# A depthwise convolution of eight channel chunks shared out anew: one chunk moves from TensorE to ScalarE and GpSimd

## The chip, the cores and the metric
The kernel runs on one core of one Trainium2 chip. A core has TensorE (PE, matrix products), VectorE (DVE), ScalarE (ACT), GpSimd (POOL) and SyncE (SP, which here only issues DMA transfers). Each engine works through its own list of instructions in order and waits on semaphores for the others. The metric is the device time of one launch in microseconds (us); three runs of the kernel before gave a median of 1120.81 us (1120.72 to 1121.36).

## The reference, cut to what matters
Two layers over x of 512 tokens by 1024 channels, in float32. Layer 0 mixes by a Conformer convolution module, layer 1 by native sparse attention; behind each stands a SwiGLU feed-forward network. What the change touches most is the convolution module:

```python
def conformer_conv_module(h, w_in, b_in, w_dw, b_dw, ln_g, ln_b, w_out):
    a, g = jnp.split(h @ w_in + b_in, 2, axis=-1)
    u = a * jax.nn.sigmoid(g)
    u = lax.conv_general_dilated(
        u, w_dw[:, None, :].astype(u.dtype), window_strides=(1,),
        padding=[(CONV_WIDTH - 1, 0)], dimension_numbers=('NWC', 'WIO', 'NWC'),
        feature_group_count=D_MODEL) + b_dw
    ...
    uf = (uf - mu) * lax.rsqrt(var + LN_EPS) * ln_g.astype(jnp.float32) + ln_b.astype(jnp.float32)
    u = jax.nn.silu(uf).astype(h.dtype)
    return u @ w_out
```

The convolution is depthwise: each of the 1024 channels has 31 taps of its own, output[t] = sum over j of w[j] u[t - 30 + j] plus a bias. Behind it stands a LayerNorm over the channels of each token (mean mu, variance var), then silu and the output product. In attention, the change touches the compressed branch: softmax of the scores against the compressed keys, times a gate, times the compressed values.

## The kernel before, in words
**Products.** A float32 product is done as three TensorE products of split operands: high part by high part, high by low, low by high. A weight tile `wr` comes by DMA from SP's queue (three buffers); ACT copies its rounded high part into `wh`, and DVE subtracts to get the low part `wl` (two buffers each). One tile of the input product is 24 matmuls into a PSUM tile `pp`.

**The convolution stage** (the first 130 us) goes over 8 chunks of 128 channels, laid out as channels by time. The loop over i from 2 to 7 is called "pass i" below. A pass finishes chunk i-1 and computes the input product of chunk i:
- `glu_1(i - 1)`: DVE multiplies the gate half out of PSUM by the RMS factors (`gr`), ACT takes its sigmoid in place, DVE does the same to the other half (`ar`);
- `w_lo(n + 1)`: DVE's `wl` for the second half of this pass; `w_hi` is ACT's `wh`;
- `glu_2(i - 1)`: DVE makes the chunk u = (ar + bias) * gr;
- TensorE multiplies two tiles: `pA` (linear half) and `pG` (gate half) of chunk i.

**The depthwise part has two ways.** Chunks 0 and 1 (`DVE_CONV`) are done by DVE, one instruction per tap, accumulating in a PSUM tile `cv`; the list `TAPS_AT` says how many taps go where in each pass. Chunks 2 to 7 (`PE_CONV`) are done by TensorE: `u` is written to a DRAM buffer `swap` and read back by phase (`uf`, SP's queue), multiplied by banded tap matrices `bd` (80 matmuls a chunk, `cpe`), corrected by `nb` (made on POOL), evicted into `uf` by DVE, squared by ACT and sent back through `swap`. The bands of the first three PE chunks are loaded by POOL's DMA queue at the start (two transfers of 1280 KB each), those of the last three made on POOL by `make_band` (8 instructions of 128x640 each, `bd<-i,wtab`). There are three buffers of bands. In pass 6 TensorE does the bands of chunks 2 and 3, in pass 7 chunk 4, behind the loop chunks 5, 6 and 7.

**LayerNorm sums** run over the channels, so TensorE makes them: `ln_shift` takes the mean of chunk 0 as a shift `s` that all chunks subtract first (`u<-u,s`); `ln_sum` (`lnst`) sums the chunks in time layout and their squares (`lsq`), `ph_sum` and `ph_last` (`lng`) those in phase layout.

**What sets the order.** `pe(...)` fixes an instruction's place in its engine's list, so in this stage each engine works in the order in which the code is written. All of these instructions pass through one helper, so the profile has one line, L153, for nearly everything; they are told apart by their tiles.

**Attention.** `cmp_k` makes the compressed keys and copies four small pieces `kcb` on DVE. `soft_c` finishes the softmax of the first pair of heads: DVE's sum (`cl<-sc`), a reciprocal, the product with the gates (`cl<-cl,gates`) and POOL's scaling (`sc<-sc,cl`). `V_BESIDE` is a table that says which small steps stand beside which block of the value product; `weigh` scales the probabilities `Pm`, mostly on POOL.

Of the kernel before, what the change touches and what calls it, by code (L numbers as in the profile page):

```python
# [19 lines left out]
P = 128  # L20
# [35 lines left out]
PE_CONV = (2, 3, 4, 5, 6, 7)  # L56
LN_ORDER = (0, 1)
BAND_BUFS = 3
LOADED = 3
SPLIT = {7: 2}  # L60
EH = 2
TAPS_AT = {2: (2, 4), 3: (3, 5), 4: (3, 5), 5: (3, 5), 6: (7, 3, 3), 7: (4, 6, 0), 8: (5, 4)}
NLN = len(LN_ORDER)
PH_B = 48
NPH = PH_B + 8 * len(PE_CONV)
# [26 lines left out]
    (("ga", "w", "s0", "s1 b1"), ("", "s2 s3 w", "gb s4 l", "s5 st1"), ("s6 l", "s7 l", "sc", "")))  # L92
# [85 lines left out]
def trunk(ctx: ExitStack, tc: tile.TileContext, A, out):  # L178
# [132 lines left out]
    wtab = cb.tile([P, len(PE_CONV) - LOADED, 320], F32, name="wtab")  # L311
# [158 lines left out]
    def conv_module():  # L470
        acc = new_acc()
        with ExitStack() as cx:
# [112 lines left out]
            def glu_2(i, ar, gr):  # L585
# [6 lines left out]
                if i in PE_CONV[:3]:  # L592
                    ups[i] = conv_pe_load(i)
# [50 lines left out]

            def conv_nb(i):
                j = PE_CONV.index(i)
                nb = cp.tile([P, 8, 64], F32, tag="c", bufs=3, name=f"nb{i}")
                pe(nc.gpsimd.tensor_tensor(
                    nb, ph[:, PH_B + 8 * j:PH_B + 8 * j + 8].unsqueeze(2).to_broadcast([P, 8, 64]),
                    sh["sp"][:, None, :].to_broadcast([P, 8, 64]), ALU.subtract))  # L650
                sh["g", i] = ups[i][:, :, 4:], nb, SPLIT.get(i, 8)
# [13 lines left out]
            def conv_end(i, ps):  # L665
                conv_nb(i)
# [23 lines left out]
            def ln_stat(i):  # L690
                pe(nc.vector.tensor_tensor(vch[i], vt[i], sh["s"], ALU.subtract))
# [20 lines left out]
            def ph_last():  # L712
                ps = sh["G2"] = pm.tile([P, 64], F32, tag="pm", name="lng")
                for g in range(8):
                    for j in (4, 5):
# [8 lines left out]
            def ln_rows():  # L724
                sh["rows"] = ct.tile([P, 8, 64], F32, tag="ptap", name="rows", bufs=3)
# [20 lines left out]
            def ln_end():  # L746

                red = sh["red"]
                pe(nc.vector.tensor_tensor(red, red, sh["G2"], ALU.add))
# [27 lines left out]
            for i in range(2, NK):  # L777
# [4 lines left out]
                glu_2(i - 1, *z)  # L782
                if i == 6:
                    ps = [conv_mm(2, 0, 8)]
                    make_band(3)
                    ps.append(conv_mm(3, 0, 8))
                    taps(c[0])
                    ln_shift(LN_ORDER[0])
                elif i == 7:
                    make_band(4)  # L790
                    for j in range(2):
                        ph_sum(j)
                        ups[5 + j] = conv_pe_load(5 + j)
# [1705 lines left out]
```

## Time and profile before

| | |
|---|---|
| median of three runs | 1120.81 us (1120.72 to 1121.36) |
| the profiled execution | 1120.53 us, its span 1118.8 us, granted TensorE clock 1.00 |
| busy in the span | PE 1111.2 us (99%), DVE 847.1 (76%), ACT 612.8 (55%), POOL 389.9 (35%) |
| convolution stage, chain of waits from 59.93 to 127.66 us | PE pp 47.3%, PE cpe 42.7%, PE lng 4.6%, rest 5.4% |
| POOL in that stage | 24 instructions of `make_band`, 76.1 to 115.8 us; idle from 18 us to 76 us but for its transfers |

A row of the timeline or of the chain reads: start in us, length in us, engine, line, operation, output tile <- input tiles, shape, count, and in brackets the idle time before it with what ended it. A row with x8 is eight instructions in a run. PE records carry modelled ends, so their lengths overlap; the steps between their starts are the pace. In a row of the tiles' view three numbers stand for the shortest, median and longest duration in ns.

### The profile page before, as it was taken

How to read it: one execution, taken by the hardware profiler on the slowest of the kernel's cores; microseconds unless marked ns; L12 is line 12 of the kernel's file. 1: busy time of each engine (PE TensorE's matmuls, PEld its weight loads, DVE VectorE, ACT ScalarE, POOL GpSimd, SP SyncE). 2: the span in 40 equal slices, each digit the busy share in tenths (PEclk: the TensorE clock that was granted, in tenths of full speed). 3: DMA queues.
4: the chain of work that ended last, by engine and by line, in shares of the span. 5: the costliest groups of instructions: out<-in, count | busy, mean ns of one | idle time of the engine just before them, and what ended most of it. 6: DMA issues, size and time to landing. Idle time of an engine off the chain costs nothing.

```text
span 1118.8 us, 21723 instructions
## 1 busy us (share of the span) xinstructions
PE 1111.2 (99%) x8350; PEld 998.1 (89%) x8350; DVE 847.1 (76%) x1569; ACT 612.8 (55%) x1120; POOL 389.9 (35%) x431
## 2 busy tenths in 40 slices
PE   9999999999999999999999999999999999999998
PEld 6888788999999988998789877768889999998898
DVE  7997897998766578875677878764799876657676
ACT  6322475566555465555344688774556655545543
POOL 1029242024444200333243678752302454420041
PEclk9999999999999999999999999999999999999999
DMA  9744428277877532534373132112736787762342
GB/s 361 290 137 126 106 94 226 101 194 210 205 196 199 160 123 95 152 102 116 119 176 116 53 80 54 40 40 94 209 111 177 205 214 197 197 180 96 111 133 76
DMA packets 86551, 164.26 MB, mean 147 GB/s; under 512 B 36656, under 2 KB 37808, under 8 KB 85680
## 3 DMA queue, kind: packets, MB, share of 16 engines
q1 hardware_dynamic: 66800, 108.47, 31.0%
q0 software_dynamic: 19504, 54.37, 20.5%
q8 instruction: 65, 1.06, 0.4%
q14 instruction: 38, 0.31, 0.1%
q10 hardware_dynamic: 144, 0.04, 0.0%
HBM read 147.22 MB, written 5.28 MB: 136 GB/s over the span
## 4 chain that ended last, share of the span: by engine, by line
PE 94%; DVE 3%; ACT 1%; issue 1%; POOL 0%; DMA 0%; SPq 0%; DVEq 0%; POOLq 0%; ACTq 0%
PE st L153 50%; PE pp L153 28%; PE O L153 4%; PE T L153 3%; PE cpe L153 3%; PE S L153 3%; PE pv L153 2%; PE psc L153 1%; DVE Pm L153 1%; ACT hh L153 0%; DMA x<-xT 0%; DVE t L153 0%; PE z L153 0%; DVE wl L153 0%; POOL Pm L153 0%
## 5 line engine op out<-in xcount | busy, mean ns | idle before, releaser
L153 PE MATMUL st<-ball,sh 128*128 128x256 f32 x1760 | 299.7, 275 | 0.0
L153 PEld LDWEIGHTS st<-ball,sh 128*128 128x128 f32 x1760 | 267.5, 192 | 0.3
L153 PE MATMUL st<-ball,sl 128*128 128x256 f32 x880 | 242.3, 275 | 0.0
L153 DVE TENSOR_TENSOR wl<-wr,wh 128x1024 fp32r<-128x1024 f32 (+3 forms) x143 | 178.0, 1245 | 66.3 <-ACT wh L153 66.0
L153 ACT ACTIVATE wh<-wr 128x1024 fp32r<-128x1024 f32 (+4 forms) x144 | 148.6, 1032 | 143.9 <-PE pp L153 57.4
L153 POOL DMA_DIRECT2D S<-fw_x x88 | 78.1, 893 | 279.8 <-DVE sl L153 195.9
L153 PEld LDWEIGHTS st<-ball,sl 128*128 128x128 f32 x880 | 169.2, 192 | 0.0
L153 POOL TENSOR_TENSOR S<-S,wr 128x512 f32<-128x512 f32 x72 | 99.9, 1388 | 142.5 <-DMA wr<-fw_op 115.6
L153 PE MATMUL pp<-hh,wh 128*128 128x512 f32 x384 | 148.8, 388 | 0.1
L153 PE MATMUL pp<-hh,wl 128*128 128x512 f32 x384 | 146.2, 381 | 0.4 <-DVE wl L153 0.3
L153 PE MATMUL pp<-hl,wh 128*128 128x512 f32 x384 | 145.6, 380 | 0.1
L153 ACT ACTIVATE sh<-S 128x512 fp32r<-128x512 f32 x176 | 101.7, 622 | 69.1 <-PE st L153 59.7
L153 DVE TENSOR_TENSOR sl<-S,sh 128x512 fp32r<-128x512 f32 x176 | 114.2, 686 | 19.3 <-ACT sh L153 16.1
L153 PE MATMUL st<-ball,wh 128*128 128x256 f32 x704 | 122.5, 275 | 0.0
L153 PEld LDWEIGHTS st<-ball,wh 128*128 128x128 f32 x704 | 107.2, 192 | 0.2
L153 PE MATMUL st<-row,wh 128*128 128x512 f32 x352 | 104.7, 379 | 0.0
L153 PE MATMUL st<-ball,wl 128*128 128x256 f32 x352 | 96.9, 275 | 0.0
L153 ACT ACTIVATE c<-st 128x256 f32<-128x256 f32 x132 | 50.1, 381 | 70.8 <-PE st L153 44.4
L153 POOL TENSOR_SCALAR Pm<-Pm,mx,gates 128x512 f32<-128x512 f32 (+2 forms) x112 | 70.8, 644 | 40.4 <-DVE mx L153 20.1
L153 PEld LDWEIGHTS pp<-hh,wh 128*128 128x128 f32 x384 | 72.8, 190 | 13.3 <-issue 2.3
L153 PEld LDWEIGHTS pp<-hh,wl 128*128 128x128 f32 x384 | 73.0, 190 | 11.9 <-DVE wl L153 1.7
L153 PEld LDWEIGHTS pp<-hl,wh 128*128 128x128 f32 x384 | 72.8, 190 | 10.2 <-DVE hl L153 0.5
(274 smaller groups left out, 2174.6 us busy)
## 6 DMA issues: line engine op xcount, KB each, us to landing
S<-fw_x POOLq DMA_DIRECT2D x88, 512.0 KB, 6.0
wr<-fw_in SPq DMA_DIRECT2D x44, 512.0 KB
wr<-fw_or SPq DMA_DIRECT2D x28, 512.0 KB
r<-fw_x SPq DMA_DIRECT2D x44, 256.0 KB
bd<-bands POOLq DMA_DIRECT2D x6, 1280.0 KB, 16.2
wr<-cw_in SPq DMA_DIRECT2D x14, 512.0 KB
wr<-fw_s SPq DMA_DIRECT2D x8, 512.0 KB
wr<-fw_op SPq DMA_DIRECT2D x8, 512.0 KB
```

What stands on the lines that cost most here:

```text
L153: z = f(*a, **kw)
```

## The change
Chunk 2 leaves TensorE: `PE_CONV` has five chunks (3 to 7), and chunk 2 is done by ACT and POOL together. For each tap ACT multiplies u of chunk 2 by the tap's weights into one of three buffers `pt` (the first product, with the bias, starts the sum `pacc`), and POOL adds it: `pacc<-pacc,pt`, 30 times. `POOL_TAPS` spreads the 31 taps over passes 3 (4 and 4), 4 (4 and 4), 5 (4 and 4) and 6 (7).

With it, in the convolution stage: four bands are loaded instead of three (`LOADED`), the fourth, for chunk 6, issued on POOL's queue in pass 6, and only the band of chunk 7 is made on POOL. Pass 6 does the bands of chunks 3 and 4 one after the other, pass 7 none. `TAPS_AT` puts 12 taps instead of 7 into pass 6, 6 instead of 10 into pass 7 and 8 instead of 9 behind the loop. The subtraction and square of chunk 0 (`ln_stat`) stand in pass 6, ahead of that pass's weight split; chunk 2's are made on POOL and ACT. The `nb` of a chunk are all made in one go in `conv_nb`, apart from the eviction. `ph_last` sums one chunk instead of two (16 matmuls instead of 32), `ln_sum` three instead of two.

In attention: the four `kcb` copies are on ACT; the sum and reciprocal of `soft_c` become `soft_b`, placed earlier, and the rest of it is placed right behind the gates ("gb"), ahead of the `Pm` scalings; of two late scalings the second is done first ("l2").

**ACT, passes 3 to 6**, from the sigmoid of chunk 2 (`gr_482`) on; `wh` is a weight's high part, `s` the evicted shift. Before:

```order
L153 ACTIVATE gr_482<-gr_482,vec 128x512
L153 ACTIVATE wh_526<-wr_449 128x1024
L153 ACTIVATE wh_562<-wr_497 128x1024
L153 ACTIVATE gr_565<-gr_565,vec 128x512
L153 ACTIVATE wh_607<-wr_531 128x1024
L153 ACTIVATE wh_643<-wr_578 128x1024
L153 ACTIVATE gr_646<-gr_646,vec 128x512
```

The same stretch now (`u_145` is chunk 2, `wdw` the taps):

```order
L156 ACTIVATE gr_482<-gr_482,vec 128x512
L156 ACTIVATE pacc<-u_145,vec,wdw 128x512
L156 ACTIVATE pt<-u_145,wdw 128x512 x3
L156 ACTIVATE wh_530<-wr_449 128x1024
L156 ACTIVATE pt<-u_145,wdw 128x512 x4
L156 ACTIVATE wh_578<-wr_501 128x1024
L156 ACTIVATE gr_581<-gr_581,vec 128x512
L156 ACTIVATE pt<-u_145,wdw 128x512 x4
L156 ACTIVATE wh_637<-wr_547 128x1024
```

Each weight split and each sigmoid of these passes now stands behind four products (in pass 6 the shift's eviction behind seven).

**POOL, from the last band transfer of the start on**; `i_108` is an identity, `wtab` the taps from which bands are made. Before:

```order
L153 DMA bd_306<-bands 128x2560 x2
L153 ISA
L153 TENSOR_TENSOR bd_815<-i_108,wtab 128x640 x8
L153 TENSOR_TENSOR nb_957<-ph,sp 128x512
L153 TENSOR_TENSOR nb_964<-ph,sp 128x512
L153 TENSOR_TENSOR bd_1009<-i_108,wtab 128x640 x8
```

Now:

```order
L156 DMA bd_306<-bands 128x2560 x2
L156 ISA
L156 TENSOR_TENSOR pacc<-pacc,pt 128x512 x30
L156 DMA bd_988<-bands 128x2560 x2
L156 TENSOR_TENSOR nb_1014<-ph,sp 128x512
L156 TENSOR_TENSOR nb_1016<-ph,sp 128x512
L156 TENSOR_TENSOR nb_1018<-ph,sp 128x512
L156 TENSOR_TENSOR u_145<-pacc,s 128x512
```

The 30 sums stand where POOL had nothing before, the fourth band's transfers behind them, and two of the three runs of band making are gone.

**DVE, pass 6**, from u of chunk 5 (`u_148`) on; `u_143` is chunk 0, `cv` chunk 1's sum. Before:

```order
L153 SCALAR_TENSOR_TENSOR u_148<-ar_730,vec,gr_727 128x64x8
L153 SCALAR_TENSOR_TENSOR u_143<-u_143,wdw,cv_441 128x512
L153 TENSOR_SCALAR cv_906<-u_144,wdw,vec 128x512
L153 SCALAR_TENSOR_TENSOR cv_906<-u_144,wdw,cv_906 128x512 x8
L153 TENSOR_TENSOR wl_954<-wr_693,wh_953 128x1024
L153 TENSOR_TENSOR uf_489<-cpe_734,nb_957 128x8x64
```

Now:

```order
L156 SCALAR_TENSOR_TENSOR u_148<-ar_796,vec,gr_793 128x64x8
L156 SCALAR_TENSOR_TENSOR u_143<-u_143,wdw,cv_441 128x512
L156 TENSOR_SCALAR cv_992<-u_144,wdw,vec 128x512
L156 SCALAR_TENSOR_TENSOR cv_992<-u_144,wdw,cv_992 128x512 x13
L156 TENSOR_TENSOR u_143<-u_143,s 128x512
L156 TENSOR_TENSOR wl_1054<-wr_759,wh_1053 128x1024
L156 TENSOR_TENSOR uf_588<-cpe_826,nb_1014 128x8x64
```

Five more taps and chunk 0's subtraction stand ahead of the weight's low part and of the first eviction `uf`.

The diff, cut to its core:

```diff
-PE_CONV = (2, 3, 4, 5, 6, 7)
-LN_ORDER = (0, 1)
+PE_CONV = (3, 4, 5, 6, 7)
+POOL_CONV = 2
+POOL_TAPS = {3: (4, 4), 4: (4, 4), 5: (4, 4), 6: (7,)}
+LN_ORDER = (0, 2, 1)
 BAND_BUFS = 3
-LOADED = 3
+LOADED = 4
+PTAP_BUFS = 3
 SPLIT = {7: 2}
 EH = 2
-TAPS_AT = {2: (2, 4), 3: (3, 5), 4: (3, 5), 5: (3, 5), 6: (7, 3, 3), 7: (4, 6, 0), 8: (5, 4)}
+TAPS_AT = {2: (2, 4), 3: (3, 5), 4: (3, 5), 5: (3, 5), 6: (12, 3, 3), 7: (3, 3), 8: (2, 6)}
 NLN = len(LN_ORDER)
 PH_B = 48
-NPH = PH_B + 8 * len(PE_CONV)
+NPH = PH_B + 48
...
-    (("ga", "w", "s0", "s1 b1"), ("", "s2 s3 w", "gb s4 l", "s5 st1"), ("s6 l", "s7 l", "sc", "")))
+    (("ga", "w", "s0", "s1 sb b1"), ("", "s2 s3 w", "gb sc s4 l", "s5 st1"), ("s6 l2", "s7 l", "", "")))
...
-                if i in PE_CONV[:3]:
+                if i in PE_CONV[:4]:
...
+            def pool_tap_list():
+                c = sh["pc"] = ct.tile([P, T], F32, tag="pacc", name="pacc", bufs=1)
+                for j in range(TAPS):
+                    z = u[POOL_CONV][:, 2 + j:2 + j + T]
+                    if j == 0:
+                        yield pe(nc.scalar.activation(c, z, AF.Identity, scale=wtap(POOL_CONV, 0),
+                                                      bias=v(V_BDW + POOL_CONV)))
+                    else:
+                        t = ct.tile([P, T], F32, tag="ptap", name="pt", bufs=PTAP_BUFS)
+                        pe(nc.scalar.activation(t, z, AF.Copy, scale=wtap(POOL_CONV, j)))
+                        yield pe(nc.gpsimd.tensor_tensor(c, c, t, ALU.add))
+
+            pool_tap = pool_tap_list()
+
+            def pool_taps(n):
+                for _ in range(n):
+                    next(pool_tap, None)
...
+            nbs = {}
+
             def conv_nb(i):
                 j = PE_CONV.index(i)
-                nb = cp.tile([P, 8, 64], F32, tag="c", bufs=3, name=f"nb{i}")
+                nb = nbs[i] = cp.tile([P, 8, 64], F32, tag="c", bufs=3, name=f"nb{i}")
...
+                vt[POOL_CONV] = sh["pc"]
+                eng = nc.gpsimd if i == POOL_CONV else nc.vector
+                pe(eng.tensor_tensor(vch[i], vt[i], sh["s"], ALU.subtract))
...
                 glu_2(i - 1, *z)
+                if i in POOL_TAPS:
+                    pool_taps(POOL_TAPS[i][0])
                 if i == 6:
-                    ps = [conv_mm(2, 0, 8)]
-                    make_band(3)
-                    ps.append(conv_mm(3, 0, 8))
+                    ps = [conv_mm(3, 0, 8), conv_mm(4, 0, 8)]
+                    load_band(3)
                     taps(c[0])
                     ln_shift(LN_ORDER[0])
+                    for j in range(3):
+                        conv_nb(PE_CONV[j])
                 elif i == 7:
-                    make_band(4)
                     for j in range(2):
                         ph_sum(j)
-                        ups[5 + j] = conv_pe_load(5 + j)
-                    ps = [conv_mm(4, 0, 8)]
+                        conv_nb(PE_CONV[3 + j])
+                    make_band(4)
                     taps(c[0])
                 pA = proj_tile(pm, "pm")
-                taps(c[-2])
+                if i != 7:
+                    taps(c[-2])
+                if i == 6:
+                    q = [ln_stat(LN_ORDER[0])]
                 w_hi(n + 2)
                 w_lo(n + 2)
+                if i in POOL_TAPS:
+                    pool_taps(sum(POOL_TAPS[i][1:]))
                 if i == 6:
-                    conv_end(2, ps[0])
-                    conv_end(3, ps[1])
-                elif i == 7:
-                    conv_end(4, ps[0])
-                    make_band(5)
-                    q = [ln_stat(LN_ORDER[0])]
+                    conv_end(3, ps[0])
+                    conv_end(4, ps[1])
+                    q.append(ln_stat(LN_ORDER[1]))
                 pG = proj_tile(pm, "pm")
                 taps(c[-1])
             z = glu_1(7, pA, pG)
...
             w_hi(state["next"] + 1)
             taps(TAPS_AT[8][1])
-            def ph_mid():
-                ph_sum(2)
-                ph_sum(3)
-
-            ps = conv_mm(6, 0, 8, mid=(5, ph_mid))
-            q.append(ln_stat(LN_ORDER[1]))
+            def ln_mid():
+                ln_sum(0, q[0])
+                ln_sum(1, q[1])
...
+            ps = conv_mm(6, 0, 8, mid=(5, ln_mid))
+            q.append(ln_stat(LN_ORDER[2]))
             sh["w"] = pc.tile([P, T], F32, tag="pc", name="warm")
             conv_end(6, ps)
-            conv_nb(7)
+            conv_at(7)
             n = SPLIT[7]
             for g0 in range(0, 8, n):
                 ps = conv_mm(7, g0, n)
                 conv_ev(7, ps, g0, n)
                 if g0 == 0:
                     w_lo(state["next"] + 1)
-                    ln_sum(0, q[0])
-                    ln_sum(1, q[1])
+                    ph_sum(2)
+                    ph_sum(3)
                 elif g0 == n:
                     ph_red()
+                    ln_sum(2, q[2])
...
-                    nc.vector.tensor_copy(kc[par * 64:par * 64 + 64, par * 32:par * 32 + 32],
-                                          pk[par * 64:par * 64 + 64, :32])
+                    nc.scalar.activation(kc[par * 64:par * 64 + 64, par * 32:par * 32 + 32],
+                                         pk[par * 64:par * 64 + 64, :32], AF.Copy)
...
+            def soft_b():
+                l = box["cl"] = qk.tile([P, 16], F32, tag="cl", name=nm("cl"), bufs=1)
+                nc.vector.tensor_reduce(l, sc.rearrange("p t j (h n) -> p (t j h) n", h=2), AX.X, ALU.add)
+                nc.vector.reciprocal(l, l)
+
             def soft_c():
                 s3 = sc.rearrange("p t j (h n) -> p (t j h) n", h=2)
-                l = qk.tile([P, 16], F32, tag="cl", name=nm("cl"), bufs=1)
-                nc.vector.tensor_reduce(l, s3, AX.X, ALU.add)
-                nc.vector.reciprocal(l, l)
+                l = box["cl"]
...
+        extra["l2"] = lambda: weigh(*late.pop(1))
```

More of the change, by code (lines that the diff above doesn't have):

```diff
@@ L310, in trunk @@
     wdw = cb.tile([P, NK * TAPS + EDGE + ASIDE], F32, name="wdw")[:, :NK * TAPS]
-    wtab = cb.tile([P, len(PE_CONV) - LOADED, 320], F32, name="wtab")
+    wtab = cb.tile([P, 3, 320], F32, name="wtab")[:, :len(PE_CONV) - LOADED]
     i16 = cb.tile([P, 16], F32, name="i16")
@@ L650, in conv_nb, with conv_at @@
                     sh["sp"][:, None, :].to_broadcast([P, 8, 64]), ALU.subtract))
+            def conv_at(i):
+                nb = nbs[i]
                 sh["g", i] = ups[i][:, :, 4:], nb, SPLIT.get(i, 8)
@@ L665, in conv_end @@
             def conv_end(i, ps):
-                conv_nb(i)
+                conv_at(i)
                 conv_ev(i, ps, 0, 8)
@@ L690, in ln_stat @@
             def ln_stat(i):
-                pe(nc.vector.tensor_tensor(vch[i], vt[i], sh["s"], ALU.subtract))
+                vt[POOL_CONV] = sh["pc"]
+                eng = nc.gpsimd if i == POOL_CONV else nc.vector
+                pe(eng.tensor_tensor(vch[i], vt[i], sh["s"], ALU.subtract))
                 q = ct.tile([P, T], F32, tag="A", name=f"lsq{i}", bufs=3)
@@ L714, in ph_last @@
                 for g in range(8):
-                    for j in (4, 5):
+                    for j in (4,):
                         for e, z in enumerate(sh["g", PE_CONV[j]][:2]):
@@ L724, in ln_rows @@
             def ln_rows():
-                sh["rows"] = ct.tile([P, 8, 64], F32, tag="ptap", name="rows", bufs=3)
+                sh["rows"] = ct.tile([P, 8, 64], F32, tag="ptap", name="rows", bufs=PTAP_BUFS)
                 pe(nc.scalar.activation(sh["rows"], by_phase(sh["ps"]), AF.Copy))
@@ L748, in ln_end @@
                 red = sh["red"]
-                pe(nc.vector.tensor_tensor(red, red, sh["G2"], ALU.add))
+                pe(nc.vector.tensor_tensor(red[:64], red[:64], sh["G2"][:64], ALU.add))
                 ln_tok()
@@ L1903, in q_pair @@
             if p == 0:
-                return move, scores, stacks, soft_a, soft_c, trans
+                return move, scores, stacks, soft_a, soft_b, soft_c, trans
             return [lambda: (move(0), scores(0)), lambda: (stacks(0), scores(1)),
                     soft_a if p < 3 else lambda: (move(1), soft_a()),
-                    lambda: stacks(1), soft_c, trans, lambda: move(1)]
+                    lambda: stacks(1), lambda: (soft_b(), soft_c()), trans, lambda: move(1)]
         extra, bcs = {}, {}
@@ L1968, in first_pair @@
         def first_pair():
-            move, scores, stacks, soft_a, soft_c, trans = q_pair(0)
+            move, scores, stacks, soft_a, soft_b, soft_c, trans = q_pair(0)
             extra.update(p0=lambda: scores(0), p1=lambda: scores(1), st0=lambda: stacks(0), st1=lambda: stacks(1),
-                         p2m=lambda: move(1), sa=soft_a, sc=soft_c, tr0=trans)
+                         p2m=lambda: move(1), sa=soft_a, sb=soft_b, sc=soft_c, tr0=trans)
             move(0)
```

## The prediction, made before the result was known
> **What bounds the kernel now.** I read the page first, then the chain of waits, then the windows and timelines of the convolution stage, then the tiles.
>
> ```profile
> span 1118.8 us, 21723 instructions
> PE 1111.2 (99%) x8350; PEld 998.1 (89%) x8350; DVE 847.1 (76%) x1569; ACT 612.8 (55%) x1120; POOL 389.9 (35%) x431
> PE 94%; DVE 3%; ACT 1%; issue 1%; POOL 0%; DMA 0%; SPq 0%; DVEq 0%; POOLq 0%; ACTq 0%
> ```
>
> TensorE sets the end: whatever is taken from it counts, unless a wait takes its place. The chain through the convolution stage shows the same place by place (start, length, what):
>
> ```profile
> 93.06 1.00 PE lng L153 x8
> 94.06 4.82 PE cpe L153 x160
> 98.88 10.56 PE pp L153 x48
> ...
> 118.74 2.48 PE cpe L153 x80
> 121.22 1.04 PE lnst L153 x8
> ...
> 125.91 1.15 PE lng L153 x64
> ```
>
> PE goes from one block to the next. But it has little in reserve against DVE, as pass 5 shows (columns: length, PE, PEld, DVE, ACT, POOL):
>
> ```profile
> 61.67:72.16 10.49, 10.49 (x80) 9.05 (x81) 10.28 (x15) 2.84 (x3) 0.00 (x0) 1.00 0.55 171
> ```
>
> DVE is busy 10.28 of 10.49 us, ACT 2.84, POOL not at all. A pass in which DVE does the same work and waits a little more is longer than 10.49.
>
> **What leaves PE.** Chunk 2's bands go (-4.82, the row at 94.06), and so does half of the last sums (-1.15/2 = -0.58); one more pair of lnst matmuls comes (half of the 1.04, +0.52). Together -4.88 us, if nothing else moves.
>
> **What the sums cost on POOL.** No row shows `pacc<-pacc,pt`. Nearest are the sums in place of two full 128x512 tiles elsewhere in the kernel (the numbers of the first row are ns, shortest, median, longest), and the making of bands, which reads broadcasts:
>
> ```profile
> L153 POOL TENSOR_TENSOR S<-S,wr x72: 1270/1290/2146, 248.8 to 1099.0; 128x512 f32<-128x512 f32 x72
> 303.67 2.65 POOL L153 TENSOR_TENSOR S<-S,wr 128x512 f32<-128x512 f32 x2
> ...
> 76.07 9.90 POOL L153 TENSOR_TENSOR bd<-i,wtab 128x640 f32<-128x640 f32 x8 [57.87 <-PE cpe L153]
> 89.28 12.60 POOL L153 TENSOR_TENSOR bd<-i,wtab 128x640 f32<-128x640 f32 x8
> ```
>
> Two sums take 2.65 with the last lasting 1.28, so each steps on by 1.37. The new ones form a chain (each reads the `pacc` of the one before) and wait for ACT, so I take 1.37. From below stands the bands' price by element, 9.90/8/640*512 = 0.99; from above, 1.6 (12.60/8, a run beside DVE).
>
> **What POOL and DVE do to each other.** Why 9.90 us in one run and 12.60 in the other? Around 95 us:
>
> ```profile
> 93.97 1.28 POOL L153 TENSOR_TENSOR bd<-i,wtab 128x640 f32<-128x640 f32 x1
> 95.21 2.26 POOL L153 TENSOR_TENSOR bd<-i,wtab 128x640 f32<-128x640 f32 x1
> 97.43 1.99 POOL L153 TENSOR_TENSOR bd<-i,wtab 128x640 f32<-128x640 f32 x1
> ...
> 94.96 1.37 DVE L153 TENSOR_TENSOR wl<-wr,wh 128x1024 fp32r<-128x1024 f32 x1
> 96.26 2.17 DVE L153 SCALAR_TENSOR_TENSOR u<-ar,vec,gr 128x512 f32<-128x512 f32 x1
> ```
>
> and where POOL does nothing, or DVE does taps:
>
> ```profile
> 62.87 1.22 DVE L153 TENSOR_TENSOR wl<-wr,wh 128x1024 fp32r<-128x1024 f32 x1
> 74.48 1.14 DVE L153 SCALAR_TENSOR_TENSOR u<-ar,vec,gr 128x512 f32<-128x512 f32 x1
> 76.95 6.30 DVE L153 SCALAR_TENSOR_TENSOR cv<-u,wdw,cv 128x512 f32<-128x512 f32 x8
> ```
>
> Beside taps (one operand in PSUM) neither is slowed: 8 bands in 9.90, 8 taps in 6.30. Beside `wl` and `u`, which read two SBUF tiles, each waits for the other: a band goes from 1.28 to 2.26 or 1.99, `u` from 1.14 to 2.17. POOL lost 0.98 and 0.71 at these two. I take 0.7 a meeting, since some such instructions will start between two sums (bounds: 0.1, about what this `wl` lost, and 1.0).
>
> The Trainium skill, page "SBUF — State Buffer", section "Who interferes with whom", says the same: a DVE instruction with two SBUF inputs and a GpSimd instruction that reads SBUF shut each other out for their whole length, one with a single SBUF input does not. These rows agree (2.26 beside `wl`, 9.90/8 beside taps). It speaks against a change that sets 30 SBUF sums beside DVE's `wl` and `u`.
>
> **The pace of passes 4 and 5.** A pass now has 8 sums and three such DVE instructions (`wl`, `u`, `wl`): 8*1.37 + 3*0.7 = 13.06 us against 10.49. ACT can be only three products ahead (three buffers). The sigmoid and the weights' `wh` stand behind products on ACT, and DVE's `u` and `wl` wait for them with the taps and the next pass behind. So after three products ACT and DVE go at POOL's pace: +2.57 a pass. In pass 3, `wh` stands behind `pacc` and three products:
>
> ```profile
> 42.45 1.12 DVE L153 SCALAR_TENSOR_TENSOR u<-ar,vec,gr 128x512 f32<-128x512 f32 x1
> 45.12 1.06 ACT L153 ACTIVATE wh<-wr 128x1024 fp32r<-128x1024 f32 x1 [3.56 <-PE pp L153]
> 72.87 0.72 ACT L153 ACTIVATE gr<-gr,vec 128x512 f32<-128x512 f32 x1 [0.84 <-DVE gr L153]
> L153 ACT ACTIVATE sq<-x 128x512 f32<-128x512 f32 x13 | 8.0, 627 | 7.0 <-DVE x L153 3.7 <-DVE acc L153 3.3
> ```
>
> With 0.72 for `pacc` and 0.63 a product they end at 43.57+0.72+3*0.63 = 46.2, where `wh` began at 45.12: +1.0. DVE's first instruction of pass 6 (`gr`), now at 72.16, comes at about 72.16+1.0+2*2.57 = 78.3.
>
> **Where PE waits for it.** PE's own delay is smaller at first: weights are split ahead of their tile.
>
> ```profile
> 65.84 1.06 ACT L153 ACTIVATE wh<-wr 128x1024 fp32r<-128x1024 f32 x1 [2.73 <-PE pp L153]
> 72.16 0.68 DVE L153 TENSOR_TENSOR gr<-pp,Rb 128x512 f32<-128x512 f32 x1
> 75.46 0.73 DVE L153 SCALAR_TENSOR_TENSOR u<-u,wdw,cv 128x512 f32<-128x512 f32 x1
> 90.33 1.27 DVE L153 TENSOR_TENSOR uf<-cpe,nb 128x512 f32<-128x512 f32 x2
> 109.03 0.63 ACT L153 ACTIVATE lsq<-u 128x512 f32<-128x512 f32 x1 [0.45 <-DVE u L153]
> 119.73 0.71 DVE L153 TENSOR_TENSOR u<-u,s 128x512 f32<-128x512 f32 x1
> ```
>
> Pass 5: the low part at 62.87, ended 64.09, comes 1.0+2.57 later (67.7); PE ends the tile before it at 65.84 (the `wh` that waits for that tile), some 0.4 later by its modelled end: +1.4. Pass 6: the last tap of chunk 0 (75.46) is due at 82.5, and PE's `shift` is there at about 83.1: nothing, up to +1.2 if `u` meets a sum. Then PE would be at `ph_sum` (lng) at 93.06+1.4 = 94.5. That sum needs the squares of chunk 4's eviction, which stand behind this on DVE and ACT, from `gr` on: `gr` and `ar` 1.2 (twice 0.68, overlapping a little), `wl` 1.3, `u` 2.0 (2.17, with the same overlap), 15 taps at 6.30/8 = 11.8, `u<-u,s` 0.7, `lsq` 0.6 and `wh` 1.1 on ACT, `wl` 1.2, one `uf` 0.6 (the half of 1.27), and, taking a square of its tile on ACT like `lsq`, 0.6: 21.1, and 0.1 where the work goes from engine to engine: 21.2. (The second eviction goes beside the first square.) 78.3+21.2 = 99.5: PE reaches `ph_sum` 99.5-93.06 = 6.4 us later than before, 1.4 by the wait in pass 5 and 5.0 here. This is the wait that takes the place of the one chunk.
>
> From there on PE has what it had, less 4.88 us. One more wait: chunk 7's trip through DRAM.
>
> ```profile
> 110.95 1.37 DVE L153 SCALAR_TENSOR_TENSOR u<-ar,vec,gr 128x512 f32<-128x512 f32 x1 [0.19 <-ACT gr L153]
> 112.52 1.53 SPq L625 DMA_DIRECT2D swap<-u  x1
> 116.25 0.57 SPq L626 DMA_DIRECT2D uf<-swap  x1
> ```
>
> From the end of `u` (112.32) to conv 7 at 118.74+2.48/2 = 119.98 there are 7.7 us, which cover it; the second transfer's issue bounds it from below at 4.5. Now the end of the products is at 99.5+1.0+10.56 = 111.0, `u` ends 2.9 (112.32-109.43) + 0.8 for POOL's bands behind, at 114.7, and convs 5 and 6 with two pairs of sums (9.64+1.04) end at 121.7; 114.7+7.7 = 122.4. Between 0 and +0.7 by these ends, up to 1.5 if DVE lags; I take +0.6, near the upper end, since the transfers behind `uf` share SP's queue.
>
> **Costed at nothing.** The fourth band is issued behind the 30 sums, at about 45.0+30*1.37+8*0.7 = 91.7, and lands by
>
> ```profile
> DMA to landing us min/median/max: 7.5/16.2/25.6
> ```
>
> the median at 108, with conv 6 due at 111.0+4.82 = 115.8 (cover gone from 1.6 a sum on, or at the longest landing: 117.3, +1.5). The `nb` behind it come by 94 (`uf` asks for them at 97). The one band made on POOL (8*1.27 to 12.6) begins near 100 and is due at 121. Attention:
>
> ```profile
> 624.14 0.49 DVE L153 TENSOR_TENSOR cl<-cl,gates 128x16 f32<-128x16 f32 x1
> 621.46 3.78 POOL L153 TENSOR_SCALAR Pm<-Pm,mx,gates 128x512 f32<-128x512 f32 x6 [15.36 <-DVE mx L153]
> 625.22 1.04 POOL L153 TENSOR_TENSOR sc<-sc,cl 128x512 f32<-128x512 f32 x1
>   PE pct L153: 0.3, 1
> ```
>
> PE waits 0.3 for `sc`; that goes, and the `Pm` behind `sc` on POOL and behind the 0.49 on DVE come as much later; 0, bounds 0.5 either way.
>
> **The sum**: +6.4 - 4.88 + 0.6 = +2.1, on this execution's own 1120.53 (span 1118.8 and 1.7 around it), 1122.6; the median of the runs shown lies 0.28 above it, so 1122.9, say **1123 us**. With a step of 1.27 a sum (the shortest `S`), 1.8 less in passes 4 and 5 together: 1121. With 1.45 and a loss of 1.0 at each meeting, +1.3 and +1.8: 1126.
>
> **A rule with another result.** The Trainium skill, page "GPSIMD Engine Reference", section "3.1 Elementwise — side-by-side cycle accounting", has 4497 ns for a sum of 2048 float32 elements, by estimate 1.12 us for 512. The rows here (1.29 median, 1270 ns the shortest of 72) do not bear that out.
>
> **The rivals.**
> 1. *Faster: the sums hide.* If a sum meets fewer of DVE's instructions than I think, a pass is 8*1.37 = 10.96, `gr` of pass 6 at about 74.1 (72.16+1.0+2*0.47), and the path from it 20.2 (no meetings): 94.3, +1.2 - 4.88 + 0 = -3.7: 1117; with all of it hidden 1116. For it: POOL was idle, ACT busy 2.84 us a pass. Against: `u` at 2.17.
> 2. *Within 0.2%: the sums are cheap.* With 1.2 a step, a pass is 8*1.2+2.1 = 11.7, +1.2 each; `gr` at 72.16+1.0+2.4 = 75.6, `ph_sum` at 96.8: +3.7 - 4.88 + 0.3 = -0.9, 1120. For it: bands cost 0.99 for 512. Against: `S`, the same form, never under 1.27. The skill's 1.12, with 0.08 between sums, would be this rival.
> 3. *Slower still: POOL's queue.* At 1.6 a sum, 14.9 a pass, +4.4 each: `ph_sum` at 72.16+1.0+8.8+21.2 = 103.2, +10.1 - 4.88 + 0.6 = +5.8, 1126.6; from here on the fourth band and the `nb` come late too and add 1 to 3. For it: the run of 12.60. Against: DVE's taps leave POOL free most of a pass.
> 4. *The change does not do what it says*: were PE not the bound in this stage, the chunk removed would give nothing. The chain speaks against it; 1121, and not slower.
>
> **How the numbers follow.** Mine 0.55, the first 0.19, the second and fourth together 0.14 (0.02 of it faster, 0.12 the same), the third 0.12. About 0.2% (2.24 us) is what a measurement of this kernel can tell from no change, and mine lies just at that bound: of its 0.55 I give 0.29 to slower, 0.23 to the same, 0.03 to faster. Faster 0.19+0.03+0.02 = 0.24, same 0.12+0.23 = 0.35, slower 0.12+0.29 = 0.41. The likeliest alone: 1121 to 1126. For 8 in 10 the range takes in most of the first rival: 1116.8 to 1126.2.
>
> **What would show it.** POOL: 30 `pacc` back to back from 45 to about 92 us, steps of 1.3 to 1.4, some of 2 beside `wl` and `u`. ACT: products that wait for POOL. DVE: `u` at 2 us, `gr` of pass 6 near 78. PE: a gap of about 1.4 in pass 5, of about 5 ahead of `lng` near 95, none ahead of conv 6. I am wrong if `pacc` steps at 1.1, if `u` stays at 1.1, or if PE finds the squares ready near 94.5.

## The result, and the profile after

The changed kernel takes 1126.74 us (median of 6 runs, 1126.06 to 1127.74) against 1120.78 for the kernel before, measured beside it: about half a percent slower (the ratio on record is 1.0056, with a 95% interval of 1.0045 to 1.0066). The forecast was 1123, slower, with a range up to 1126.2; the loss is almost three times as large as forecast (+6.0 us instead of +2.1). The profiled execution of the changed kernel took 1126.40 us.

The span, then the chain of waits through the convolution stage (start, length, what; the chain before it goes through POOL's sums):

```profile
span 1124.6 us, 21417 instructions
```

```profile
68.99 1.89 POOL pacc L156
...
83.73 1.10 PE shift L156 x2
84.83 10.37 PE pp L156 x48
95.20 4.57 issue
99.77 3.13 PE lng L156 x8
102.89 10.78 PE pp L156 x48
113.68 8.31 PE cpe L156 x280
121.99 0.99 PE lnst L156 x8
...
125.81 1.19 PE lng L156 x8
126.99 1.32 PE cpe L156 x40
128.31 0.98 PE lnst L156 x4
129.29 2.48 PE cpe L156 x80
131.77 1.15 PE lng L156 x32
132.92 0.60 PE lnrt L156 x4
```

The chain, which before ran through TensorE from block to block, now runs through POOL's `pacc` up to 70.9 us, and TensorE stands still for 4.57 us ahead of `lng`. Set beside the chain of before, where `lnrt` starts at 127.06:

| stretch of TensorE | before | after | difference | forecast |
|---|---|---|---|---|
| start of the first `lng` | 93.06 | 99.77 | +6.7 | +6.4 |
| that `lng` | 1.00 | 3.13 | +2.1 | 0 |
| a chunk's bands in pass 7 | 4.82 | - | -4.8 | -4.8 |
| the two product tiles behind | 10.56 | 10.78 | +0.2 | 0 |
| from there to `lnrt` | 17.63 | 19.24 | +1.6 | +0.5 |

Together +5.86. Behind `lnrt` both kernels take 991.7 us to the end of the span, so the loss lies in the convolution stage and the attention edits show nothing. The +6.7 is made up of waits of TensorE for DVE: 1.4 us in passes 4 and 5 for `wl` (forecast 1.4), 1.4 ahead of `shift` for `u` (forecast nothing, at most 1.2) and 4.6 ahead of `lng` (forecast 5.0), less a pause of 0.75 in the bands of pass 6 that only the kernel before has.

The passes, by windows of all engines (columns as in the prediction; the last three are the granted TensorE clock, the busy share of the DMA engines and GB/s), and DVE's rows in pass 4:

```profile
52.02:65.22 13.20, 12.64 (x59) 10.76 (x58) 12.41 (x14) 8.07 (x12) 12.57 (x9) 1.00 0.40 120
95.20:99.77 4.57, 0.00 (x1) 0.03 (x2) 2.93 (x4) 1.65 (x3) 2.78 (x3) 1.00 1.00 426
99.77:102.89 3.12, 3.12 (x9) 0.54 (x9) 3.05 (x5) 2.62 (x4) 0.51 (x1) 0.52 0.93 274
```

```profile
54.50 2.15 DVE L156 SCALAR_TENSOR_TENSOR u<-ar,vec,gr 128x512 f32<-128x512 f32 x1
...
59.41 2.07 DVE L156 TENSOR_TENSOR wl<-wr,wh 128x1024 fp32r<-128x1024 f32 x1 [0.58 <-ACT wh L156]
```

A pass takes 13.20 us where it took 10.49 (forecast 13.06). `u` takes 2.15 (before 1.12), `wl` 1.36 and 2.07 (before 1.22), three taps 2.33 as before; `gr` of pass 6 comes at 78.41 (forecast 78.3). POOL's sums, from the tiles' view (durations in ns) and the timeline:

```profile
L156 POOL TENSOR_TENSOR pacc<-pacc,pt x30: 1276/1284/2141, 44.6 to 90.9; 128x512 f32<-128x512 f32 x30
  ACT pt L156: 16.0, 17
```

```profile
44.55 47.62 POOL L156 TENSOR_TENSOR pacc<-pacc,pt 128x512 f32<-128x512 f32 x30 [26.61 <-ACT pt L156]
92.11 1.11 POOL L156 DMA_DIRECT2D bd<-bands  x2
93.24 3.52 POOL L156 TENSOR_TENSOR nb<-ph,sp 128x512 f32<-128x512 f32 x3
```

They go from 44.6 to 92.1 without a rest, and ACT's products waited 16.0 us for them in 17 places. What `lng` waits for, in the rows of DVE, ACT and TensorE (`uf` is a chunk's eviction, `nb` here its square, which ACT writes over the `nb` that the eviction has used):

```profile
98.99 1.28 DVE L156 TENSOR_TENSOR uf<-cpe,nb 128x512 f32<-128x512 f32 x2
99.70 1.23 ACT L156 ACTIVATE nb<-uf 128x512 f32<-128x512 f32 x2 [2.24 <-DVE uf L156]
100.38 1.06 PE L156 MATMUL lng<-nb,ph 128*32 128x512 f32 x1
```

`lng` starts at 99.77 on the first eviction alone. Its first matmul that reads a square starts at 100.38, and the second square ends at 100.93, with matmuls left to do behind it.

So the mechanism and its place were as forecast; what is to be explained is why a wait of the forecast length cost 3.7 us more, and whether the forecast had the right reason for the length of the pass.

### The profile page after: what moved, and what is told of

Same layout as the page of the kernel before. It is cut to its first block, busy times and chain, and to the rows that moved or that the text cites. A ratio compares the mean times of both kernels' runs of the same rounds, so it can differ in the third digit from the quotient of the medians.

```text
span 1124.6 us, 21417 instructions
## 1 busy us (share of the span) xinstructions
PE 1109.7 (99%) x8162; PEld 992.5 (88%) x8162; DVE 852.8 (76%) x1564; ACT 634.4 (56%) x1155; POOL 414.2 (37%) x446
## 4 chain that ended last, share of the span: by engine, by line
PE 91%; DVE 4%; issue 2%; POOL 2%; ACT 1%; DMA 0%; SPq 0%; DVEq 0%; POOLq 0%; ACTq 0%
PE st L156 50%; PE pp L156 25%; PE O L156 4%; PE T L156 3%; PE S L156 3%; PE pv L156 2%; POOL pacc L156 2%; PE cpe L156 1%; PE psc L156 1%; DVE wl L156 1%; ACT hh L156 0%; PE lng L156 0%; DVE u L156 0%; DVE Pm L156 0%; DMA x<-xT 0%
```

## The experiments

Starts in different traces are shifted by up to 0.8 us (`gr` of pass 3 starts between 39.3 and 40.2), so lengths are compared below. Each time is a median; the ratio behind it is to the kernel before, measured beside it (1120.27 for the first four, 1120.33 for the next four, 1120.37 for the next three, 1120.62 for the last), with its 95% interval.

**Sums left out, and half of them.** The edits, in the list of taps:

```diff
-                        yield pe(nc.gpsimd.tensor_tensor(c, c, t, ALU.add))
+                        yield t if j < TAPS - 1 else pe(nc.gpsimd.tensor_tensor(c, c, t, ALU.add))
```

```diff
+                        yield pe(nc.gpsimd.tensor_tensor(c, c, t, ALU.add)) if j % 2 == 0 else t
```

> The changed kernel without 29 of the 30 sums on POOL (the products are still made, the last sum alone stays, so chunk 2's convolution is left out). My theory: ACT and DVE are late in passes 4 to 6 because POOL's sums hold them, by the chain of sums or by meeting DVE's wl and u. Then gr of pass 6 comes at about 73.2 us instead of 78.4, u takes 1.1 and wl 1.2, the PE gap ahead of lng (4.6 us) is under 1, and the time is about 1126.7 - 6.3 - 1.5 = 1119. Rival: ACT's 31 products (0.63 to 0.72 each) ahead of the sigmoids and the wh are what is late; then gr stays near 78 and the time near 1126.

> The changed kernel with every second sum left out (15 on POOL instead of 30, so half of chunk 2's taps do not count). It tells the two ways apart in which sums hold the others. If it is the pace of the chain (8*1.37 and what it loses, against 10.49 a pass), 4 sums a pass are far below it: gr of pass 6 near 73.5, time about 1119 to 1120. If it is the meetings with DVE's wl and u alone (2.0 of the 2.7 us by which passes 4 and 5 grew), about half of them stay: about 1 us a pass, gr near 75.5, ph_sum near 96.5, time about 1122 to 1123.

Without the sums 1120.82 (ratio 1.0006, 0.9997 to 1.0016); with half of them 1124.65 (1.0038, 1.0024 to 1.0053). A pass, by windows, and the first `lng` in the chain, first without the sums:

```profile
51.93:62.45 10.52, 10.52 (x51) 9.21 (x50) 10.31 (x15) 7.62 (x11) 0.00 (x0) 1.00 0.47 136
```

```profile
94.97 2.66 PE lng L156 x8
```

and with half:

```profile
51.63:63.35 11.72, 11.72 (x56) 10.27 (x55) 11.51 (x15) 7.64 (x11) 6.67 (x4) 1.00 0.45 135
```

Without sums the pass is back at 10.52, with all of ACT's products still in it (7.62 us of ACT): the products alone make nobody late. `u` takes 1.14 there. With half of the sums POOL is idle 43% of the pass, so the chain cannot hold anybody, and the pass is still 1.2 us longer, with `u` at 2.18 and the second `wl` at 1.38: that is the meetings of DVE's `u` and `wl` with sums, and it is what the second theory said of the pass.

Both times were missed, by 1.8 and by 2 us, and both kernels have a wait that the changed kernel has not. In the kernel without sums (`s` is the shift, `sp` the shift by phase, which POOL's `nb` reads):

```profile
84.41 0.33 SPq L711 DMA_DIRECT2D swap<-s  x1
91.38 0.34 SPq L713 DMA_DIRECT2D sp<-swap  x1
93.11 3.04 POOL L156 TENSOR_TENSOR nb<-ph,sp 128x512 f32<-128x512 f32 x3 [12.00 <-DMA sp<-swap]
94.18 0.69 DVE L156 TENSOR_TENSOR uf<-cpe,nb 128x512 f32<-128x512 f32 x1 [2.71 <-POOL nb L156]
```

The two halves of the shift's trip through DRAM are issued 7.0 us apart here and 9.2 with half of the sums, against 1.7 in the changed kernel (at 89.85 and 91.52). So DVE's evictions wait for `nb` 3.0 us here and 2.0 with half of the sums. With fewer sums ahead of them the transfers of the fourth band are issued at 80.0 and 83.3 instead of 92.1, and fall on the shift's trip; the DMA engines are 98% busy or more from 84 to 88 us in the kernel without sums. That these transfers are the cause fits the rows but was not tried by itself.

So these two runs tell what a pass costs, but their times carry this wait. Without it the kernel without sums would save, by estimate, the gap ahead of `lng` (1.3 us) and 1.7 of `lng`'s 2.66, that is 3.0 us, and take about 1118. The stretch from the products to `lnrt` is 19.24 us long here too, so its 1.6 us do not come from the sums on POOL.

**Five product buffers instead of three.**

```diff
-PTAP_BUFS = 3
+PTAP_BUFS = 5
```

> The changed kernel with five product buffers instead of three. If the three products that ACT can be ahead set when its lag begins, two more put it off by 2*1.37 = 2.7 us: gr of pass 6 near 75.7, time about 1123.5. If DVE's own longer wl and u fill the pass, only DVE's waits for wh (0.6 us a pass) go: gr near 77.2, time about 1125.5.

1125.94 (1.0052, 1.0037 to 1.0067). Windows, DVE and POOL of this kernel:

```profile
51.49:63.33 11.84, 11.84 (x57) 10.36 (x56) 11.63 (x15) 7.85 (x11) 11.29 (x8) 1.00 0.45 134
```

```profile
93.88 4.23 DVE L156 TENSOR_TENSOR wl<-wr,wh 128x1024 fp32r<-128x1024 f32 x1 [1.64 <-ACT wh L156]
```

```profile
92.76 3.05 POOL L156 TENSOR_TENSOR nb<-ph,sp 128x512 f32<-128x512 f32 x3
95.76 1.26 POOL L156 TENSOR_TENSOR u<-pacc,s 128x512 f32<-128x512 f32 x1
```

The pass falls to 11.84 us, of which DVE is busy 11.63, and `gr` of pass 6 comes 2.7 us earlier, as the first theory said. The time does not follow: the weight split ahead of the evictions (`wl`) now falls beside three `nb` and a sum that POOL does one after the other without a pause, and takes 4.23 us instead of 1.57. Most of what was gained in the passes is lost there.

So a pass of 13.20 is 10.5 for DVE's own work, 1.2 to 1.3 for its meetings with sums (with half the sums, or with five buffers), and 1.4 for being held by the chain at three buffers. In DVE's rows this 1.4 is 0.7 of a longer second `wl` (2.07 instead of 1.36 to 1.38) and 0.6 of waiting for its `wh`.

**The operand in PSUM.** `ar` is written back over its PSUM tile, so that `u` reads one SBUF tile instead of two:

```diff
-                ar = ct.tile([P, T], F32, tag="B", bufs=1, name=f"ar{i}")
-                pe(nc.vector.tensor_tensor(ar, pA, R, ALU.mult))
-                return ar, gr
+                pe(nc.vector.tensor_tensor(pA, pA, R, ALU.mult))
+                return pA, gr
```

> The changed kernel with ar written back over its PSUM tile, so that DVE's u has one SBUF operand (gr) and one in PSUM, like a tap. If two SBUF operands are what makes u and a sum wait for each other, u takes 1.1 to 1.2 us in passes 4 to 6 instead of 2.15, passes 4 and 5 take 12.2 to 12.5 us instead of 13.2 (with three buffers the chain of 8 sums and two meetings holds them at 8*1.37 + 2*0.8), gr of pass 6 is near 76.8 and the time near 1124.7. If the meeting has another cause (the writes, say), u stays at 2.1 and the time at 1126.7.

1124.14 (1.0034, 1.0021 to 1.0047). DVE in pass 4:

```profile
54.57 1.13 DVE L156 SCALAR_TENSOR_TENSOR u<-pp,vec,gr 128x512 f32<-128x512 f32 x1
...
58.88 2.07 DVE L156 TENSOR_TENSOR wl<-wr,wh 128x1024 fp32r<-128x1024 f32 x1 [1.01 <-ACT wh L156]
```

`u` is back at 1.13 beside the same sums, while `wl`, which still reads two SBUF tiles, keeps 2.07. The pass is 12.60 and the time 2.6 us below the changed kernel's. That for `u` it is the second SBUF operand on which DVE and POOL meet is shown by this.

**The clock behind the gap.** Seventeen matmuls of zeros stand in the gap:

```diff
+                    sh["w"] = pc.tile([P, T], F32, tag="pc", name="warm")
+                    for _ in range(17):
+                        pe(nc.tensor.matmul(sh["w"].rearrange("p (a b) -> p a b", a=4), zb,
+                                            zb[:, None, :].to_broadcast([P, 4, P]), start=True, stop=True))
                     for j in range(2):
                         ph_sum(j)
...
-            sh["w"] = pc.tile([P, T], F32, tag="pc", name="warm")
```

> The changed kernel with 17 small matmuls of zeros in the gap of TensorE ahead of lng (they go to a PSUM tile that nobody reads). If lng takes 3.13 us since the clock is at 0.52 behind the gap of 4.6 us, the granted clock stays at 1.00, lng goes to 2.0 to 2.2 (the second square is still waited for), the products behind from 10.78 to 10.56, and the time to about 1125.6. If lng waits for the squares alone, nothing changes: 1126.7.

1125.78 (1.0049, 1.0032 to 1.0066). Windows of the rest of the gap, of `lng` and of the products, and DVE's subtraction ahead of them:

```profile
98.56:101.31 2.75, 0.00 (x0) 0.03 (x1) 1.92 (x3) 0.86 (x2) 0.00 (x0) 1.00 0.51 216
101.31:103.57 2.26, 2.26 (x9) 0.46 (x9) 2.19 (x4) 2.26 (x4) 0.00 (x0) 1.00 0.82 224
103.57:114.13 10.56, 10.56 (x51) 8.99 (x52) 10.42 (x12) 2.15 (x3) 8.71 (x7) 1.00 0.73 177
```

```profile
94.18 3.57 DVE L156 TENSOR_TENSOR u<-u,s 128x512 f32<-128x512 f32 x1
```

With TensorE kept at work the granted clock is 1.00 where it was 0.52; `lng` takes 2.26 instead of 3.12 and the products 10.56 instead of 10.78. That is 1.1 us of the loss by these two lengths; the two times' intervals overlap, so the time by itself does not tell it. The profiled execution does not tell it either: at 1127.33 us it is the slowest of the four, its `u<-u,s` took 3.57 us beside POOL's `nb` instead of 1.34, and `lng` starts 1.5 us later than in the changed kernel. The other 1.26 us of `lng` over the 1.00 of before is the wait for the squares: it starts on the first eviction, and the second square is there 1.2 us later.

**Attention alone.** The kernel before with the change's attention edits:

> The kernel before with the attention part of the change alone (copies on ACT, the split of the scaling, the order of the late scalings). By the prediction it is worth 0, within 0.5 us either way: 1120.3 to 1121.3. The rival is that it hides a loss or a gain of more than that beside the convolution's.

1120.33 (1.0001, 0.9992 to 1.0010): nothing, as forecast.

**The order.** Two steps are moved: the weight split ahead of chunk 0's subtraction, the sums of chunks 3 and 4 behind the first product tile of pass 7.

```diff
-                    for j in range(2):
-                        ph_sum(j)
-                        conv_nb(PE_CONV[3 + j])
-                    make_band(4)
                     taps(c[0])
                 pA = proj_tile(pm, "pm")
+                if i == 7:
+                    for j in range(2):
+                        ph_sum(j)
+                        conv_nb(PE_CONV[3 + j])
+                    make_band(4)
...
-                if i == 6:
-                    q = [ln_stat(LN_ORDER[0])]
                 w_hi(n + 2)
                 w_lo(n + 2)
+                if i == 6:
+                    q = [ln_stat(LN_ORDER[0])]
```

> The changed kernel with two of its steps in another order: in pass 6 the weight split stands ahead of chunk 0's subtraction and square, and in pass 7 the sums of chunks 3 and 4 behind the first product tile instead of ahead of it. If the wait ahead of lng is what costs, TensorE's first tile of pass 7 starts when its wl is there, at about 96.2 instead of 102.9, the sums then find their squares: with the 1.0 of the sums behind, about 1126.7 - 4.5 = 1122. If DVE has no time left behind (it is busy to the end of chunk 1's taps at 124), half of that comes back as a wait at the second tile or at the last sums: 1124.5.

1125.70 (1.0050, 1.0035 to 1.0065): 1 us, where 2 or 4.5 was expected. TensorE's waits, and DVE's split:

```profile
PE pp L156 <- ACT lsq L156: 4.8, 1, 4.8
```

```profile
94.61 4.10 DVE L156 TENSOR_TENSOR wl<-wr,wh 128x1024 fp32r<-128x1024 f32 x1
98.63 0.68 DVE L156 TENSOR_TENSOR u<-u,s 128x512 f32<-128x512 f32 x1
99.23 1.27 DVE L156 TENSOR_TENSOR uf<-cpe,nb 128x512 f32<-128x512 f32 x2
```

The wait moved from `lng` to the products. The row names ACT's `lsq`, but the tile that the first product needs is by the code the PSUM tile of chunk 3, and its eviction `uf` stands on DVE behind a `wl` of 4.10 us, again beside POOL's `nb`. The products start 2.8 us earlier than in the changed kernel, but now they stand behind the gap: the clock is at 0.53 from 100.05 to 103.60, and the first tile takes 7.04 us instead of 5.28. With the sums' 1.0 behind it, nearly all of the 2.8 is gone in this trace.

**All of it together**, with six product buffers and the last sums regrouped: chunk 5's are taken with chunk 1's, which is the last in `LN_ORDER` (the expectation below calls it chunk 2), and chunk 6's with chunk 7's, so that each pass fills four groups of output partitions. The core of the regrouping (the groups' rows and the first and last marks of each sum change with it):

```diff
-                    for j in (4,):
+                    for j in (3, 4):
...
                 if g0 == 0:
                     w_lo(state["next"] + 1)
-                    ph_sum(2)
-                    ph_sum(3)
                 elif g0 == n:
-                    ph_red()
-                    ln_sum(2, q[2])
+                    ph_sum(2)
+                    ln_sum(2, q[2])
+                    ph_red()
                     ln_rows()
```

> The order of e7_order, ar in PSUM as in e5_ar_psum, six product buffers, and the last sums regrouped so that each pass of TensorE over them fills four groups of columns (chunk 5's with chunk 2's, chunk 6's with chunk 7's). By my sum of the parts: 3 from the passes, 4.5 from the order, 1.0 from the sums, less 1 for DVE's rest: about 1118 to 1119, below both kernels. If POOL's and DVE's work together set the end of the stage, 1121 to 1123.

1122.79 (1.0024, 1.0014 to 1.0034), 4 us below the changed kernel and still above the one before. DVE and TensorE's wait:

```profile
91.51 4.87 DVE L156 TENSOR_TENSOR u<-u,s 128x512 f32<-128x512 f32 x1
96.30 1.27 DVE L156 TENSOR_TENSOR uf<-cpe,nb 128x512 f32<-128x512 f32 x2
```

```profile
PE pp L156 <- ACT lsq L156: 5.2, 1, 5.2
```

```profile
97.12 7.88 PE pp L156 x24
```

Now `u<-u,s` meets the `nb`, and the evictions stand behind it. The first tile behind the gap takes 7.88 us instead of 5.28: its first 4.9 us are at clock 0.50. The regrouping does what it should: chunk 5's and chunk 1's sums take 1.0 us together (in the changed kernel 1.19 and 0.98).

**Evictions first**, that is, chunk 0's subtraction behind them; the same with `ar` in SBUF and five buffers; and the kernel before with `ar` in PSUM alone:

```diff
-                if i == 6:
-                    q = [ln_stat(LN_ORDER[0])]
                 if i in POOL_TAPS:
                     pool_taps(sum(POOL_TAPS[i][1:]))
                 if i == 6:
                     conv_end(3, ps[0])
                     conv_end(4, ps[1])
+                    q = [ln_stat(LN_ORDER[0])]
```

> e8_all with chunk 0's subtraction and square behind the evictions of chunks 3 and 4 instead of ahead of them. In e8_all TensorE waited 5.2 us for the PSUM tile of chunk 3, whose eviction stood on DVE behind that subtraction, which took 4.87 us beside three nb and a sum on POOL. If this wait is the last one, the eviction comes at about 92.7 instead of 96.3, TensorE waits 1 us or less, and the time goes from 1122.8 to about 1118.5, below both kernels. If the end of the stage hangs on chunk 7's trip through DRAM or on DVE's last taps, half of it comes back: 1120.5.

> e9_evict with ar in SBUF again and five product buffers. If DVE's u with two SBUF operands is worth 1 us a pass beside the sums, passes 4 and 5 take 11.8 us instead of 11.25 or so and u of chunks 6 and 7 2.1 beside the band making: 2 us more than e9_evict. If the order alone decides, the same time as e9_evict.

> The kernel before with ar in PSUM alone. TensorE does not wait for u there; if that holds, 1120.3 within 0.5 us, and what e9_evict gains is not this edit's by itself. If u beside the bands of passes 6 and 7 (2.17 us) holds the kernel before too, 1119 to 1119.5.

1120.98 (1.0005, 0.9996 to 1.0013), 1124.09 (1.0031, 1.0019 to 1.0043) and 1120.25 (0.9998, 0.9989 to 1.0007). The PSUM operand, with the sixth buffer for which it makes room, is worth 3 us beside sums on POOL; in the kernel before it is worth nothing. Not all of the 3 us is in the passes, which differ by 0.6 each (11.26 and 11.86): TensorE's gap in pass 7 is 1.69 us in the first kernel and 2.69 in the second, and in the second the clock falls to 0.50 from 96.6 to 99.9, in the first it stays at 1.00. The first kernel has reached the time of the one before; more than half of what was expected came back as another wait. TensorE's waits, and SP's issues:

```profile
PE cpe L156 <- DMA uf<-swap: 3.5, 2, 2.4
PE pp L156 <- DVE uf L156: 1.7, 1, 1.7
```

```profile
101.69 1.27 SPq L688 DMA_DIRECT2D u<-swap  x2
103.05 0.53 SPq L264 DMA_DIRECT2D wr<-cw_os  x1
103.63 1.32 SPq L645 DMA_DIRECT2D swap<-u  x1
```

Chunk 6's way out, whose `u` is there at 101.7, is issued at 103.63, behind two transfers that nobody needs before the end of the stage.

**The queue.** These two go behind chunk 7's:

```diff
                 conv_ev(i, ps, 0, 8)
-                conv_back(i)
+                if i > 4:
+                    conv_back(i)
...
+            ups[7] = conv_pe_load(7)
+            conv_back(3)
+            conv_back(4)
             for k in range(18, 21):
                 w_dma(k)
-            ups[7] = conv_pe_load(7)
```

The edit does one thing more than its expectation says: chunk 7's own transfers now stand ahead of three loads of weights (`w_dma`).

> e9_evict with the transfers that bring chunks 3 and 4 back (u<-swap) behind chunk 7's on SP's queue instead of ahead of chunk 6's. In e9_evict TensorE waited 3.5 us for chunks' uf<-swap in two places; chunk 6's way out (swap<-u) was issued 1.9 us after u was made, behind those two transfers. If the queue's order makes them late, the two waits together go under 1.5 us and the time from 1121.0 to about 1119, below the kernel before. If the trip itself (about 7 us from u to uf) is what is late, the waits and the time stay within 0.5 us.

1118.24 (median of 11), ratio to the kernel before 0.9979 with an interval of 0.9970 to 0.9988: below both kernels by more than the measurement's uncertainty. TensorE's waits:

```profile
PE cpe L156 <- DMA uf<-swap: 0.3, 1, 0.3
```

The queue's order was what made them late: chunk 6 was behind the two transfers back (its wait of 2.4 us is gone), and chunk 7's way out, whose `u` was there at 109.87, behind a load of weights to 111.40 (its wait goes from 1.1 to 0.3). With these edits the new split of the convolution is worth 2.4 us. The regrouped sums and the queue's order were not tried in the kernel before, whose longest pause of TensorE in this stage is 0.75 us. The gain had been covered by a row of waits, each of which appeared when the one ahead of it was gone: the pace of the passes, the squares, chunk 3's PSUM tile, the transfers' queue; and behind each gap of over 3 us stood a slower clock.

## Why the prediction was wrong

**Right: what leaves and what comes.** The bands give 4.82 us; attention is worth nothing (1120.33 against 1120.27); the fourth band and the one made on POOL are not waited for.

**Right: the price of a sum and of a meeting.** 1.28 us each, in steps of 1.37; two operands in SBUF are what meets (`u` 2.15, with one in PSUM 1.13). The Trainium skill's rule that the prediction quoted from the page "SBUF — State Buffer", section "Who interferes with whom", agrees with both numbers. The rate for GpSimd's elementwise sums that the prediction took from the Trainium skill's page "GPSIMD Engine Reference", section "3.1 Elementwise — side-by-side cycle accounting", would by estimate have made it 1.12 and does not agree with 1.28. (In the prediction's lower bound, a step of 1.27 saves 2*8*0.1 = 1.6 us and not 1.8; 1121 stays.)

**Right in size, with the reason half right: the pace.** 13.06 was forecast, 13.20 measured. The prediction had ACT and DVE go at POOL's pace. That holds at three buffers, but only for the last 1.4 of the 2.7 us: with five buffers, or with half of the sums, DVE's own meetings make a pass of 11.7 to 11.8.

**Wrong: "one `uf` 0.6 ... The second eviction goes beside the first square."** This ends the path at the first square, at 99.5, and lets `lng` take its old 1.0. `lng` did start at 99.77, but on the eviction alone; the first square came 0.6 us behind that, since the path took 21.9 us instead of 21.2 (`u<-u,s` met POOL's `nb`: 1.34 instead of 0.7). The 15 taps on this path are right: pass 6 has 18 taps, 13 before, and three of them stand behind it. That 6.7 comes so near to 6.4 is luck: two errors of 0.6 to 0.7 us cancel. `lng` needs the second chunk's square as well, and the gap itself has a price: the clock is at 0.52 behind it. `lng` took 3.13, the products 0.22 more. These 2.3 us are the largest term that was missing. The Trainium skill has both halves of the second one on its page "TensorE: Matmul & The Clock Gate", section "HAM oscillation — how this bites in real kernels": no idle gaps over about 3.4 us, and half the rate behind one. The trace agrees: 4.57 us of gap, then 0.52; in the kernel with the seventeen matmuls, 2.75 us of gap, then 1.00. The length alone does not tell it: in the kernel with the evictions first and `ar` in SBUF the clock fell behind a gap of only 2.69 us, from 1.2 us after its end, to 0.50 for 3.3 us.

**Wrong: "so does half of the last sums (-1.15/2 = -0.58); one more pair of lnst matmuls comes (half of the 1.04, +0.52)".** Matmuls into different groups of 32 output partitions go side by side: `lng` takes 1.15 with 32 records as it did with 64, `lnst` 0.98 with 4 as 1.04 with 8, and the regrouped sums of two chunks 1.0. Nothing is saved and 0.98 comes, so this term is +0.98 instead of -0.06; the other sums take 0.2 more, and bands cut into more pieces 0.4. Counting matmuls was the error; the column tiles had to be read from the kernel's lines (`r0 = 64 * (n % 2) + 32 * e`).

**Not borne out: chunk 7's trip, +0.6.** In the changed kernel 0.12 us of issue stands in its place. It became a wait only when ones ahead of it were shorter: 0.8 us with `ar` in PSUM, 1.1 with the evictions first (the other 2.4 there are chunk 6's).

The sum with these terms: 6.7 + 2.1 + 0.2 - 4.8 + 1.6 = 5.8 instead of 2.1.

**The rivals.** The first (sums that hide: 1117) is not refuted by the kernel without sums: its 1120.82 has 3.0 us of the shift's trip in it, and the estimate without them, about 1118, is near 1117. But the sums did not hide. The third (slower by POOL's queue, 1126.6) came nearest in time, for a reason that did not happen: sums of 1.6 us.

## What to carry to other kernels

Work that was moved to GpSimd cost VectorE time here wherever its instruction read two SBUF tiles; putting one operand of `u` in PSUM took that away (2.15 to 1.13 us). A wait on TensorE is to be priced with what follows it: the operand that comes last, and the clock behind a gap of several us (1.1 us where the sums stood first behind it, 1.8 and 2.6 where products did). A kernel with a part left out can have a wait of its own: without the sums the two halves of the shift's trip stood 7.0 us apart instead of 1.7. And where matmuls fill only some output partitions, the price goes by the passes and not by their number, so an added sum is free only if a pass has room for it.

## What the runs showed of the hardware that was not expected

- VectorE against back-to-back work on GpSimd. Against the chain of sums, which steps with 0.08 us between two, a `wl` took 1.36 to 2.07 us. Against three `nb` and a sum with no such pause (92.8 to 97.0) one `wl` took 4.23, and in three other kernels `wl` 4.10 and `u<-u,s` 4.87 and 3.57: one instruction waited for most or all of the row. It does not always: in the changed kernel's own trace `u<-u,s` started at 94.51 beside the same row and took 1.34. What decides it, the missing pause or the moment of its start, was not tried by itself.
- Gaps of 3.77 to 6.80 us on TensorE were each followed by 3 us or more at about half of its clock (4.57 us: 0.52 for 3.1 us). Of the shorter ones, those of 1.31, 1.69 and 2.75 us were not, and one of 2.69 us was, from 1.2 us after its end.
- A trip of 32 KB through DRAM had its two halves issued 7.0 and 9.2 us apart where the two transfers of 1280 KB that load a band were issued just ahead of it, and 1.7 where they were not.
